# Hybrid decoder layer, gate/up stage: five blocks with four summed weight pairs, residual rows parked in HBM

## The chip, the cores and the metric

One core of a Trainium2 chip runs the whole layer in one launch. The metric is device time in microseconds; before the change it is 1085.96 us (median of 3 runs, 1085.82 to 1085.98).

## The reference

One decoder layer on x (256 tokens x 2048), everything in fp32:

```
u = RMSNorm(h)
lru_x, lru_gate, q, k, v, ret_gate = split(u @ W_in)          # 2048 x 6144
y = concat(RG-LRU(conv(lru_x)) * gelu(lru_gate),
           GroupNorm(retention(rope(q), rope(k), v)) * silu(ret_gate))
h = h + y @ W_out                                             # 2048 x 2048
h = h + (silu(u2 @ W_gate) * (u2 @ W_up)) @ W_down            # u2 = RMSNorm(h); 2048 x 5632 twice, 5632 x 2048
return RMSNorm(h)
```

With 256 tokens the layer is matrix products: 50 million weights are read once, and each product of two fp32 numbers is made of three TensorE products (hi x hi, hi x lo, lo x hi), for which every weight is split on the chip into a hi part (fp32r) and a lo part.

## The kernel before, in words

The kernel works off a list `program` of steps. Each step has weight units and a function that emits its matmuls. A loop at the end emits, ahead of each step, the loads of the steps to come (three loads ahead, `AHEAD`); `defer(n, f)` emits f after n further steps, `tick` counts them, one per step, empty steps included. What is emitted is then ordered per engine by a planner that works with a simulated timeline, so matmuls of neighbouring steps mix.

A load (512 KB, 128 x 1024) goes by SyncE's DMA queue into one of 6 `raw` buffers. `split` then makes the hi part (ScalarE cast, L112) and the lo part (VectorE subtraction, L113) in one of 4 `wh` and 4 `wl` buffers (or in tiles of 128 x 512 out of a pool of 60, `act_tile`).

From the output projection on (blocks 0 and 1), through gate/up (blocks 2 to 12, 512 columns of gate and the same of up each) to the down projection, a block holds four sums in four PSUM banks: c11, c12 (tokens 0 to 127 with the left and right 512 columns), c21, c22 (tokens 128 to 255). The 2048 rows of the weights come as 8 pairs of 128-row tiles. A pair is a 2 x 2 product, [a11 a12; a21 a22] with [b11 b12; b21 b22], and is done in one of two ways:

- plain, step "p": `EIGHT`, eight products of three matmuls (24 matmuls of 128 x 512), two loads;
- summed: seven products after Strassen and Winograd, of sums of activations (`Left`: s1 to s4) and sums of weights (t1 to t4, four VectorE sums per pair in `add`, L648). They are done apart: step "s" (`share`, two loads, 12 matmuls) for the products p1, p5, p6, p7, which are summed over the pairs, during the block before; step "d" (`direct`, one load of the second half again, 9 matmuls) in the block itself.

When the last pair is shared, L781 to L787 combine the four sums once per block: p1 is copied to a tile (ScalarE, L782), p and q are formed (VectorE, L783, L784), q goes to c12 (ScalarE, L785), and c22 and c21 are corrected (L786, L787). `direct` and `plain` then accumulate on these banks. `SUMMED` says which pairs of each block are summed, `STEPS` the order of its steps: the s steps in a block's string are the next block's pairs. The last step of a block ends its banks with `post`: silu and product (`ffn_post`, L842, L844), and the result is transposed on TensorE in the first step of the next block (`turn`, L833), for block 12 two steps later by `defer`.

The residual rows h (`htok`, 8 tiles of 128 x 512) are completed in blocks 0 and 1 by `out_post` (L585, L586) and stay in SBUF (`resid`) until the down projection adds to them (`into`, L888). The final norm's weights are loaded on SyncE's queue (`load_fw`, L861) into four `late` tiles. PSUM has two pools of four banks (`bank`, `aux`), used by odd and even blocks in turn (`room`).

## Time and profile before

| | before |
|---|---|
| runs, us | 1085.96 (1085.82 to 1085.98) |
| profiled execution: span from the first to the last instruction, us | 1084.4 |
| TensorE matmul busy | 1074.2 us, 99% |
| TensorE weight load busy | 899.5 us, 83% |
| VectorE busy | 953.5 us, 88% |
| ScalarE busy | 660.9 us, 61% |
| GpSimd busy | 51.0 us, 5% |
| HBM read, written | 235.26 MB, 2.10 MB |

The page gives the profiled execution's own time only as this span; the runs' median is 1.5 us above it. Rows begin with the engine or the line; an arrow points from the operands to the result; "x850" is a count. PE is TensorE, PEld its weight load, DVE VectorE, ACT ScalarE, POOL GpSimd, SP SyncE; a trailing q is the engine's queue. A matmul's own row is longer than its share of the pipeline, so what one costs is read from the starts of its neighbours.

### The profile page before, as it was taken

The page shows a single profiled execution, that of the slowest core. Times are in us where ns is not written, and L with a number is a line of the kernel's source. Part 1 is how long each engine was busy: PE and PEld are TensorE (multiplying, and loading weights), DVE is VectorE, ACT ScalarE, POOL GpSimd, SP SyncE. Part 2 cuts the span into 40 slices and gives each one's busy share as a digit, 9 for nine tenths or more (in the row PEclk, how much of TensorE's full clock was granted, in tenths as well). Part 3 has the DMA queues.
Part 4 walks back from the last instruction along what each step waited for, and adds up shares of the span by engine and source line. Part 5 has one row for each costly group of instructions (what it writes and reads, how often), then busy time and mean ns, then how long its engine had stood idle before and what let it go on. Part 6 is the DMA issues. An engine that isn't in the chain of part 4 may idle for free.

```text
span 1084.4 us, 14584 instructions
## 1 busy us (share of the span) xinstructions
PE 1074.2 (99%) x5101; PEld 899.5 (83%) x5101; DVE 953.5 (88%) x1371; ACT 660.9 (61%) x935; POOL 51.0 (5%) x61
## 2 busy tenths in 40 slices
PE   9999999999999999999999999999999999999997
PEld 7888888888888788888888888888888888888885
DVE  7789799988878889888998998999899899898986
ACT  7666644468746676565566566556556666655563
POOL 0612230000000000000000000000000000000001
PEclk9999999999999999999999999999999999999999
DMA  9964474444565567577677677686675756465652
GB/s 330 333 211 168 160 252 173 174 175 171 181 230 205 184 228 275 198 248 266 220 245 261 220 264 235 233 289 214 233 271 194 265 181 213 171 214 199 212 209 85
DMA packets 69274, 238.32 MB, mean 220 GB/s; under 512 B 7888, under 2 KB 8272, under 8 KB 69200
## 3 DMA queue, kind: packets, MB, share of 16 engines
q1 hardware_dynamic: 68400, 235.29, 62.7%
q0 software_dynamic: 512, 1.57, 0.4%
q8 instruction: 40, 0.66, 0.2%
q10 hardware_dynamic: 288, 0.52, 0.1%
q14 instruction: 34, 0.28, 0.1%
HBM read 235.26 MB, written 2.10 MB: 219 GB/s over the span
## 4 chain that ended last, share of the span: by engine, by line
PE 97%; DVE 1%; issue 1%; DMA 0%; ACT 0%; POOL 0%; SPq 0%; POOLq 0%; ACTq 0%
PE c L670 22%; PE c L672 22%; PE c L671 22%; PE fm L184 11%; PE fm L186 5%; PE tm L164 3%; PE tm L165 3%; PE tm L166 3%; PE p L672 1%; PE p L671 1%; PE p L670 1%; PE ft L833 1%; DMA raw<-in_w_v 0%; PE ht L576 0%; PE sc L482 0%
## 5 line engine op out<-in xcount | busy, mean ns | idle before, releaser
L112 ACT CAST wh<-raw 128x1024 fp32r<-128x1024 f32 (+1 forms) x490 | 460.9, 965 | 362.6 <-PE c L672 132.5
L113 DVE TENSOR_TENSOR wl<-raw,wh 128x1024 fp32r<-128x1024 f32 (+1 forms) x490 | 538.2, 1122 | 91.2 <-ACT wh L112 88.4
L671 PE MATMUL c<-wl,ah 128*128 128x512 f32 x850 | 331.0, 390 | 0.0
L672 PE MATMUL c<-wh,al 128*128 128x512 f32 x850 | 330.4, 389 | 0.0
L670 PE MATMUL c<-wh,ah 128*128 128x512 f32 x850 | 275.0, 391 | 0.2 <-ACT wh L112 0.2
L670 PEld LDWEIGHTS c<-wh,ah 128*128 128x128 f32 x850 | 159.4, 188 | 33.4 <-ACT wh L112 1.1
L672 PEld LDWEIGHTS c<-wh,al 128*128 128x128 f32 x850 | 159.6, 188 | 33.0
L671 PEld LDWEIGHTS c<-wl,ah 128*128 128x128 f32 x850 | 159.6, 188 | 32.7
L184 PE MATMUL fm<-u,wh 128*128 128x512 f32 x512 | 161.3, 396 | 0.0
L186 PEld LDWEIGHTS fm<-u,wl 128*128 128x128 f32 x512 | 96.0, 188 | 22.5
L186 PE MATMUL fm<-u,wl 128*128 128x256 f32 x512 | 101.1, 278 | 0.0
L184 PEld LDWEIGHTS fm<-u,wh 128*128 128x128 f32 x512 | 78.4, 189 | 0.3
L648 DVE TENSOR_TENSOR raw<-raw,raw 128x512 f32<-128x512 f32 x106 | 73.1, 690 | 2.8
L648 DVE TENSOR_TENSOR raw<-raw 128x512 f32<-128x512 f32 x106 | 72.7, 689 | 2.4
L671 PE MATMUL c<-wl,sh 128*128 128x512 f32 x176 | 68.5, 389 | 0.0
L672 PE MATMUL c<-wh,sl 128*128 128x512 f32 x176 | 68.0, 389 | 0.0
L670 PE MATMUL c<-wh,sh 128*128 128x512 f32 x176 | 60.4, 394 | 0.3 <-ACT sh L112 0.3
L165 PE MATMUL tm<-wl,u 128*128 128x512 f32 x128 | 48.8, 394 | 0.0
L166 PE MATMUL tm<-wh,u 128*128 128x512 f32 x128 | 48.7, 390 | 0.0
L164 PE MATMUL tm<-wh,u 128*128 128x512 f32 x128 | 47.3, 398 | 0.8 <-ACT u L288 0.8
L954 POOL TENSOR_TENSOR htok<-htok,fw 128x512 f32<-128x512 f32 x2 | 2.5, 1273 | 895.9 <-ACT junk L947 895.9
L670 PEld LDWEIGHTS c<-wh,sh 128*128 128x128 f32 x176 | 33.1, 188 | 7.3 <-ACT sh L112 0.7
(245 smaller groups left out, 1034.9 us busy)
## 6 DMA issues: line engine op xcount, KB each, us to landing
raw<-in_w_gu SPq DMA_DIRECT2D x212, 512.0 KB, 5.5
raw<-in_w_down SPq DMA_DIRECT2D x91, 512.0 KB, 4.3
raw<-in_w_out SPq DMA_DIRECT2D x34, 512.0 KB, 3.7
raw<-in_w_lx SPq DMA_DIRECT2D x16, 512.0 KB, 6.3
raw<-in_w_k SPq DMA_DIRECT2D x16, 512.0 KB, 3.5
raw<-in_w_q SPq DMA_DIRECT2D x16, 512.0 KB, 4.0
raw<-in_w_rg SPq DMA_DIRECT2D x16, 512.0 KB, 3.4
raw<-in_w_lg SPq DMA_DIRECT2D x16, 512.0 KB, 3.4
```

Of the source, the lines that this page charges most:

```text
L112: act.copy(out=dst_h, in_=src)
L113: v.tensor_tensor(out=dst_l, in0=src, in1=dst_h.bitcast(F32), op=ALU.subtract)
L164: pe.matmul(ps, ah, wh, start=first, stop=False)
L165: pe.matmul(ps, ah, wl, start=False, stop=False)
L166: pe.matmul(ps, al, wh, start=False, stop=last)
L184: pe.matmul(ps, wh, hl, start=n + i == 0, stop=False)
L186: pe.matmul(ps[:, :S], wl, hl[:, :S], start=False, stop=n + i == len(order) - 1)
L648: v.tensor_tensor(out=dst, in0=a, in1=b, op=ALU.add)
L670: pe.matmul(p, ah, bh, start=first, stop=False, skip_group_check=onto)
L671: pe.matmul(p, ah, bl, start=False, stop=False, skip_group_check=onto)
L672: pe.matmul(p, al, bh, start=False, stop=last, skip_group_check=onto)
L833: pe.transpose(pt[:, o : o + P], g[:, (2 * b + c) * P : (2 * b + c) * P + P], ident)
```

## The change

1. `SUMMED` and `STEPS`: blocks 4 to 8 have four summed pairs each (before, blocks 4, 6, 8 and 10 had four and the others three); blocks 4 to 7 run 4 p, 4 s and 4 d.
2. In those five blocks (`KEEP`) b11 and t2 are split into act tiles. `share` builds p1 in c22 (a11 x b11), copies it from there into c11's bank, which is one that a transposition of an earlier block wrote (`spare`), adds all pairs' s2 x t2 on top in c22 at the end, and combines with three VectorE sums and ScalarE copies. `share_apart` is the old way for the others.
3. s2 changes its sign (L552), and with it the forms of L783 and L898.
4. The four sums of a shared pair are no longer made together: the first at the load, the other three one by one with the next loads (`pending`).
5. The eight residual rows are written to HBM by ScalarE's queue in `out_post`; the `resid` pool and two others are closed ahead of block 3 (before: two pools, ahead of block 2) and six more raw buffers take the place, used every second load until block 12. After block 12 the rows come back, and the final norm's weights come, both on GpSimd's queue.
6. Transposes in gate/up set the accumulation flag on the first of a bank's four only.

```diff
-SUMMED = ((), (4, 5), (2, 3)) + ((1, 2, 3), (0, 1, 2, 3)) * 4 + ((1, 2, 3), (1, 2, 3))
+SUMMED = ((), (4, 5), (2, 3)) + ((1, 2, 3),) + ((0, 1, 2, 3),) * 5 + ((1, 2, 3), (0, 1, 2, 3), (1, 2, 3), (1, 2, 3))
-STEPS = ("pppspppspp", "ppspdpsdpp", "pdpsdpspspp") + ("pspsdpsdpsdp", "psdpsdpsddp") * 4 + ("psdpsdpsdpp", "psdpsdpsdpp")
+STEPS = ("pppspppspp", "ppspdpsdpp", "pdpsdpspspp") + ("pspsdpsdpsdp",) + ("psdpsdpsdsdp",) * 4 + ("psdpsdpsddp", "pspsdpsdpsdp", "psdpsdpsddp", "psdpsdpsdpp", "psdpsdpsdpp")
+KEEP = tuple(range(4, 9))
...
+    def raw_tile():
+        turn_of[0] += 1
+        pool_ = more[0] if more and turn_of[0] % 2 else rpool
+        return pool_.tile([P, 1024], F32, tag="raw", name=nm("raw"))
...
-                v.tensor_tensor(out=s2, in0=a11, in1=s1, op=ALU.add)
+                v.scalar_tensor_tensor(out=s2, in0=a11, scalar=-1.0, in1=s1, op0=ALU.mult, op1=ALU.subtract)
-                v.tensor_tensor(out=s4, in0=a12, in1=s2, op=ALU.subtract)
+                v.tensor_tensor(out=s4, in0=a12, in1=s2, op=ALU.add)
...
+            act.dma_start(out=kept[cb, t], in_=h)          # out_post, after the square
...
     class Shared(Quad):
-            self.add(r)
-            self.parts["t2"] = h[:, 512:], l[:, 512:]
-            split(*self.parts["t2"], r[:, :512])
-            self.cut(("t1", "t3"), self.ra)
             self.parts["t4"] = act_tile("t4h", F32R), act_tile("t4l", F32R)
-            split(*self.parts["t4"], r[:, 512:])
+            def first():
+                add(b11, b11, b12)
+            def second():
+                add(b12, b12, b22)
+                self.cut(("t1", "t3"), self.ra)
+            def third():
+                add(b22, b11, b22)
+                split(*self.parts["t2"], b22)
+            def fourth():
+                add(b21, b22, b21)
+                split(*self.parts["t4"], b21)
+            first()
+            pending.extend((self, f) for f in (second, third, fourth))
...
         def share(self, m):
+            ps, seed = self.ps, spare[self.index % 2]
+            if self.index not in KEEP:
+                return self.share_apart(m)
+            for c, a, b in (("c22", "a11", "b11"), ("c12", "s1", "t1"), ("c21", "s3", "t3")):
+                if m == 0:
+                    ps[c] = room(self.index)(c)
+                three(ps[c], left[a], right[b], m == 0, last)
+                if last and c == "c22":
+                    ps["c11"], spare[self.index % 2] = seed, None
+                    act.copy(out=seed, in_=ps["c22"])
+            if not last:
+                return
+            for k, i in enumerate(self.summed):
+                three(ps["c22"], self.lefts[i]["s2"], self.shared[k].parts["t2"], False, i == self.summed[-1], True)
+            p, q = act_tile("p"), act_tile("q")
+            act.activation(out=p, in_=ps["c22"], func=AF.Copy, scale=-1.0)
+            v.tensor_tensor(out=q, in0=p, in1=ps["c12"], op=ALU.subtract)
+            act.copy(out=ps["c12"], in_=q)
+            v.tensor_tensor(out=ps["c22"], in0=q, in1=ps["c21"], op=ALU.subtract)
+            v.tensor_tensor(out=ps["c21"], in0=ps["c21"], in1=p, op=ALU.subtract)
...
     def swap():
         early.close()
+        more.append(extra.enter_context(tc.tile_pool(name="raw2", bufs=6)))
+    def stop_more():                                       # ahead of block 12
+        more.clear()
+    def swap_back():                                       # after block 12
+        extra.close()
         late.append(ctx.enter_context(tc.tile_pool(name="late", bufs=4)))
+        resid[0] = ctx.enter_context(tc.tile_pool(name="resid2", bufs=8))
+        for key in [(cb, t) for cb in range(4) for t in range(2)]:
+            htok[key] = res_tile("htok")
+            pool.dma_start(out=htok[key], in_=kept[key])
+        load_fw()
...
+            if pending and pending[0][0] is not un:        # after each load
+                pending.pop(0)[1]()
+        while any(q in units for q, _ in pending):         # ahead of a step that needs them
+            pending.pop(0)[1]()
```

## Rows read from the trace of the kernel before

**Rows 1.** The page: busy line, and the chain by engine.

```profile
PE 1074.2 (99%) x5101; PEld 899.5 (83%) x5101; DVE 953.5 (88%) x1371; ACT 660.9 (61%) x935; POOL 51.0 (5%) x61
...
PE 97%; DVE 1%; issue 1%; DMA 0%; ACT 0%; POOL 0%; SPq 0%; POOLq 0%; ACTq 0%
```

**Rows 2.** Waits of PE: waiter <- cause: total us, times, longest.

```profile
PE warm L105 <- DVE eps_t L98: 1.1, 1, 1.1
...
PE c L670 <- ACT sh L112: 0.3, 1, 0.3
```

**Rows 3.** Order of time, PE, gate/up: start us, duration us, instruction, count.

```profile
559.73 0.39 PE L671 MATMUL c<-wl,ah 128*128 128x512 f32 x1
...
562.90 0.39 PE L671 MATMUL c<-wl,ah 128*128 128x512 f32 x1
...
575.14 1.30 PE L670 MATMUL c<-wh,ah 128*128 128x512 f32 x5
```

**Rows 4.** Windows of blocks 4, 5 and 12: us, busy of each engine, clock, DMA, GB/s.

```profile
477.20:516.20 39.00, 39.00 (x177) 32.32 (x176) 34.87 (x43) 23.36 (x32) 0.00 (x0) 1.00 0.72 247
516.20:561.30 45.10, 45.10 (x204) 37.38 (x203) 41.23 (x52) 26.51 (x35) 0.00 (x0) 1.00 0.73 244
...
811.20:853.20 42.00, 42.00 (x191) 34.60 (x190) 40.20 (x57) 28.40 (x39) 0.00 (x0) 1.00 0.64 225
```

**Rows 5.** Groups by line and shape: busy us, mean ns | idle before, releasers.

```profile
L113 DVE TENSOR_TENSOR wl<-raw,wh 128x1024 fp32r<-128x1024 f32 x392 | 477.7, 1231 | 78.4 <-ACT wh L112 75.8
...
L648 DVE TENSOR_TENSOR raw<-raw,raw 128x512 f32<-128x512 f32 x106 | 73.1, 690 | 2.8
...
L113 DVE TENSOR_TENSOR wl<-raw,wh 128x512 fp32r<-128x512 f32 x98 | 66.9, 683 | 12.7 <-ACT wh L112 12.5
...
L844 DVE SCALAR_TENSOR_TENSOR gated<-c,r_tok,gated 128x512 f32<-128x512 f32 x22 | 15.8, 741 | 0.6 <-ACT gated L842 0.6
...
L783 DVE TENSOR_TENSOR p<-c,p 128x512 f32<-128x512 f32 x13 | 8.9, 684 | 0.4 <-PE c L672 0.4
```

**Rows 6.** Order of time, ACT, around a copy of p1.

```profile
836.89 3.47 ACT L112 CAST wh<-raw 128x1024 fp32r<-128x1024 f32 x4
...
840.79 0.58 ACT L782 COPY p<-c 128x512 f32<-128x512 f32 x1
```

**Rows 7.** Waits of ACT from 400 to 800 us.

```profile
ACT wh L112 <- DVE raw L648: 87.3, 33, 3.0
ACT wh L112 <- PE c L672: 71.2, 62, 2.7
...
ACT wh L112 <- DMA raw<-in_w_gu: 0.2, 1, 0.2
```

**Rows 8.** DMA issues: ACT's (order of time), POOL's, and the gate/up loads (us to landing).

```profile
1079.31 0.88 ACTq L986 DMA_DIRECT2D out<-htok  x2
...
L441 POOL DMA_DIRECT2D decay<-in_decay x8: 556/562/772, 140.0 to 143.9; - x8
...
raw<-in_w_gu SPq DMA_DIRECT2D x212, 512.0 KB, 5.5
```

**Rows 9.** Order of time: PE near 370 and near 948 us.

```profile
370.41 0.50 PE L670 MATMUL c<-wh,ah 128*128 128x512 f32 x1
...
371.78 0.39 PE L671 MATMUL c<-wl,sh 128*128 128x512 f32 x1
...
947.95 0.39 PE L672 MATMUL p<-wh,sl 128*128 128x512 f32 x1
...
950.20 0.40 PE L671 MATMUL p<-wl,sh 128*128 128x512 f32 x1
```

**Rows 10.** Line L888: duration ns min/median/max, first and last start.

```profile
L888 DVE TENSOR_TENSOR htok<-htok,part x8: 680/682/685, 953.6 to 1062.5; 128x512 f32<-128x512 f32 x8
```

**Rows 11.** Order of time after block 12: its last products, and their transposes.

```profile
854.59 1.40 DVE L844 SCALAR_TENSOR_TENSOR gated<-c,r_tok,gated 128x512 f32<-128x512 f32 x2
...
859.76 0.38 PE L833 MATMUL ft<-ident,gated 128*128 128x128 f32 x2
```

More of the change, by code (lines that the diff above doesn't have):

```diff
@@ L124, in load @@
         def load(self, j):
-            raw = rpool.tile([P, 1024], F32, tag="raw", name=nm("raw"))
+            raw = raw_tile()
             h = wpool.tile([P, 1024], F32R, tag="wh", name=nm("wh"))
@@ L146, in part @@
             return self.h[j][:, o : o + cw], self.l[j][:, o : o + cw]
-    halfway = []
+    halfway, pending = [], []
     program = []
@@ L566, in tile_hymba_layer @@
     turns = []
+    kept = nc.dram_tensor("kept_rows", (4, 2, P, 512), F32, kind="Internal").ap()
     def out_post(d):
@@ L626, in load @@
         def load(self, half):
-            r = rpool.tile([P, 1024], F32, tag="raw", name=nm("raw"))
+            r = raw_tile()
             nc.sync.dma_start(out=r, in_=self.src[:, half * 1024 : half * 1024 + 1024])
@@ L721, in block, with transposes @@
         program.append((quads[n:], end))
+    spare = [None, None]
+    def transposes(pt, parts):
+        for n, x in enumerate(parts):
+            pe.matmul(
+                pt[:, n * P : n * P + P], x, ident, start=n == 0, stop=True, is_transpose=True, skip_group_check=n > 0
+            )
     class Shared(Quad):
-        hl = None, None
+        keep = False
         def load(self, half):
-            r = rpool.tile([P, 1024], F32, tag="raw", name=nm("raw"))
+            r = raw_tile()
             nc.sync.dma_start(out=r, in_=self.src[:, half * 1024 : half * 1024 + 1024])
@@ L732, in load, with add @@
                 self.before()
-            h, l = self.hl
             if half == 0:
                 self.ra = r
-                h, l = self.hl = [wpool.tile([P, 1024], F32R, tag=g, name=nm(g)) for g in ("wh", "wl")]
-                self.parts["b11"] = h[:, :512], l[:, :512]
+                if self.keep:
+                    self.parts["b11"] = act_tile("b11h", F32R), act_tile("b11l", F32R)
+                else:
+                    h, l = (wpool.tile([P, 1024], F32R, tag=g, name=nm(g)) for g in ("wh", "wl"))
+                    self.parts["b11"], self.parts["t2"] = ((h[:, c : c + 512], l[:, c : c + 512]) for c in (0, 512))
                 split(*self.parts["b11"], r[:, :512])
                 return
-            self.add(r)
-            self.parts["t2"] = h[:, 512:], l[:, 512:]
-            split(*self.parts["t2"], r[:, :512])
-            self.cut(("t1", "t3"), self.ra)
+            if self.keep:
+                self.parts["t2"] = act_tile("t2h", F32R), act_tile("t2l", F32R)
             self.parts["t4"] = act_tile("t4h", F32R), act_tile("t4l", F32R)
-            split(*self.parts["t4"], r[:, 512:])
+            b11, b12, b22, b21 = self.ra[:, :512], self.ra[:, 512:], r[:, :512], r[:, 512:]
+            def add(dst, a, b):
+                v.tensor_tensor(out=dst, in0=a, in1=b, op=ALU.add)
+            def first():
[11 more added lines that the diff above has]
+            pending.extend((self, f) for f in (second, third, fourth))
     class Direct(Quad):
@@ L756, in load @@
         def load(self, half):
-            r = rpool.tile([P, 1024], F32, tag="raw", name=nm("raw"))
+            r = raw_tile()
             nc.sync.dma_start(out=r, in_=self.src[:, 1024:2048])
@@ L768, in __init__, with share_apart @@
             self.shared = [Shared(src(i), True, before and (lambda i=i: before(i))) for i in self.summed]
+            for q in self.shared:
+                q.keep = index in KEEP
             self.ps = {}
         def share(self, m):
+            left, right, last = self.lefts[self.summed[m]], self.shared[m].parts, m == len(self.summed) - 1
+            ps, seed = self.ps, spare[self.index % 2]
[18 more added lines that the diff above has]
+            v.tensor_tensor(out=ps["c21"], in0=ps["c21"], in1=p, op=ALU.subtract)
+        def share_apart(self, m):
             left, right, last = self.lefts[self.summed[m]], self.shared[m].parts, m == len(self.summed) - 1
@@ L782, in share @@
             act.copy(out=p1, in_=ps["c11"])
-            v.tensor_tensor(out=p, in0=ps["c12"], in1=p1, op=ALU.subtract)
+            v.scalar_tensor_tensor(out=p, in0=ps["c12"], scalar=-1.0, in1=p1, op0=ALU.mult, op1=ALU.subtract)
             v.tensor_tensor(out=q, in0=p, in1=ps["c22"], op=ALU.subtract)
@@ L829, in turn @@
             pt = room(j)("ft")
-            for c in range(2):
-                for t, g in enumerate(gated):
-                    o = c * S + t * P
-                    pe.transpose(pt[:, o : o + P], g[:, (2 * b + c) * P : (2 * b + c) * P + P], ident)
+            transposes(pt, [g[:, (2 * b + c) * P : (2 * b + c) * P + P] for c in range(2) for g in gated])
+            if b and j + 4 in KEEP:
+                spare[j % 2] = pt
             ff[2 * j + b] = act_tile("ff")
```

20 lines of the change are left out of this document (12 added, 8 removed).

## The prediction

> **What bounds the kernel now.** I read the page's busy line and its chain first: TensorE is busy 99% of the span, it holds 97% of the chain that ended last, and its granted clock is 1.00, the upper of its two levels (2.4 GHz), in every window of this stage [rows 1, 4]. Busy is not peak, so I asked next who makes TensorE wait: in 1084.4 us the list names four causes, 1.1 us the longest and 0.3 us the longest at a product of the later stages [rows 2]. The order of time then shows how tightly matmuls follow each other: from 559.73 to 562.90 us there are 14 intervals, 3.17 us, 0.2265 us per matmul of 128x512 [rows 3]. The windows by gate/up block close the account. A block is a list of steps, p (24 matmuls), s (12) and d (9). One with 5 p, 4 s, 3 d has 195 matmuls and takes 45.1 us, one with 4 p, 3 s, 4 d has 168 and takes 39.0 us [rows 4]; 27 matmuls are 6.1 us, 0.226 each, and what is left over both 195 x 0.2265 = 44.2 and 168 x 0.2265 = 38.1 is 0.9 us, the eight transposes. So the time of a gate/up block is its count of matmuls, with nothing added. VectorE is second, 89.4% and 91.4% in those two blocks, ScalarE far behind [rows 4].
>
> **Two more summed pairs.** SUMMED counted per block gives 3, 4, 3, 4, 3, 4, 3, 4, 3, 3 for blocks 3 to 12 before and 3, 4, 4, 4, 4, 4, 3, 4, 3, 3 after: blocks 5 and 7 gain one pair each. A plain pair costs one p = 24 matmuls; a summed one s + d = 12 + 9 = 21. So 2 x 3 = 6 matmuls go, 6 x 0.2265 = 1.36 us, on the path. In blocks: blocks 4 to 7 are the two of rows 4 twice over, 39.0 + 45.1 + 39.0 + 45.1 = 168.2 us; four blocks of 4 p, 4 s, 4 d have 180 matmuls, 180 x 0.2265 + 0.9 = 41.7 us each, 166.8 together.
>
> On VectorE each such exchange adds four sums (4 x 0.69) and three half splits (3 x 0.68): 4.8 us. The two whole splits of p, 2 x 1.23, are replaced by those of s and d, 2 x 1.23 [rows 5]. That is 9.6 us in all, six half casts on ScalarE, and one load of 512 KB each. All of it lies beside matmuls, if VectorE has room. A 4 p, 4 s, 4 d block takes it 41.23 us less one split (1.0 by spacing to 1.23) less one combination sum (0.69), 39.3 to 39.5, or from the other block 34.87 + 2.76 + 2.05 + 1.23 - 0.69 = 40.2: 94 to 96% of 41.7 us. Is that too much? The block from 811.2 to 853.2 us already has VectorE at 40.20 of 42.0 us, 95.7%, and TensorE at 42.00 of 42.00 [rows 4]. So I cost it at nothing, and what it costs without that cover is the slower rival below.
>
> **Combination with one sum less.** In the five blocks 4 to 8 the product p1 is built in c22 and copied by ScalarE into c11's bank (instead of into a tile); the sum p1 + p6 comes out of accumulation and ScalarE's copy with scale -1 stands for VectorE's L783. VectorE saves 5 x 0.684 = 3.4 us, ScalarE gets 5 x 0.58 = 2.9 us more [rows 5, 6], TensorE's count is the same. One wait is new: the s2 x t2 matmuls of c22 must stay behind ScalarE's copy out of c22. Between them lie six matmuls (c12 and c21), 1.36 us. The copy itself is 0.58 us, but ScalarE works its queue in order, and such a copy has stood behind a run of casts that began 840.79 - 836.89 = 3.9 us before it [rows 6]. The bounds are therefore nothing (copy reached at once, or matmuls of other steps put between) and 3.9 + 0.58 - 1.36 = 3.1 us a block, 16 us in all. I take nothing, by the nearest row: in the combination of before TensorE waits for ScalarE in no gate/up block [rows 2, 4]. Queued behind it would be every later matmul.
>
> **Signs.** TENSOR_TENSOR becomes SCALAR_TENSOR_TENSOR in L552, L783 (eight blocks) and L898. At 128x512 with a PSUM operand the two kinds cost 684 and 741 ns [rows 5]: some 10 x 0.06 = 0.6 us on VectorE for the last two, at L552's quarter of the size no more each, and nothing on the path.
>
> **Sums between other work, and buffers.** The four sums of a pair ran as one group, and ScalarE waited 87.3 us for them in 400 us; for gate/up weights to land it waited 0.2 us [rows 7]. So six more raw buffers remove no wait of TensorE's; they hold what the postponed sums keep longer. Gain and loss on the path: 0, where 0.7 us is the bound for the gain (the stall at 370 us, below).
>
> **The residual rows.** Eight stores issued by ScalarE, 0.44 us each on its queue by the two stores at the end [rows 8], 3.5 us in blocks 0 and 1, and no wait, since the square ahead waited for the same sum. A gain is excluded, they only add; at the other end four of them (1.8 us) lie ahead of the chain to the stall at 370 us, so up to 1.8 us; I take 0, since ScalarE works 61% of its time [rows 1] and sits idle for sums and buffers in between [rows 7]. Coming back: 8 rows and 4 weight rows of 256 KB, issued by GpSimd at about 0.56 us each [rows 8], 6.7 us of an engine that is busy 5% in all [rows 1]. They wait for the last readers of the six buffers, early in block 12, and are needed from 953.6 us on [rows 10], more than 100 us later. They add 3.1 MB to a stretch that moves 225 GB/s at a DMA share of 0.64 [rows 4]: 5 to 14 us during which weight loads share; those land 5.5 us after issue [rows 8], and in block 12 six buffers serve them as before. Bounds 0 and 2 us, taken 0.
>
> **The empty step.** swap_back is one more step between block 12 and the down projection, so the transposes of the last gate/up tiles, put off by two steps, are emitted one step earlier. Before, their input was ready at 854.59 + 1.40 = 855.99 us and they ran at 859.76 [rows 11]. Put straight behind the last matmul of the block they would wait up to 2.6 us; I take 0: they ran 3.8 us after their input was ready, so other matmuls were at hand for that long.
>
> **Sum.** -1.36 us on the path, all else beside it: the profiled execution, span 1084.4 us, becomes 1083.0. The runs' median lies 1.5 us above that span and I carry that over: 1085.96 - 1.36 = 1084.6 us. By the Trainium skill (TensorE: Matmul & The Clock Gate, section Back-to-back issue gap) a sustained matmul of 512 columns costs about 131 ns, by which the six would be worth 0.8 us and the time an estimated 1085.2; the trace shows 0.2265 us over every such stretch, and the measurement decides.
>
> **The rivals.**
> *VectorE becomes the bound (slower).* Place: blocks 4 to 7. If VectorE can't be kept busier than the 90.4% it shows on average over the two kinds of block there, 39.8 us of work make a block of 44.0 us instead of 41.7: 4 x 2.3 - 1.4 = 7.8 us, 1093.8 us. It decides from a reachable share of 94.7% downwards (39.8 / 0.947 = 42.0 us eats the gain); at 93.5% the kernel is 0.2% slower. For it: up to five matmuls with hi parts run in a row while lo parts are being made [rows 3], and 95% with ScalarE in the loop leaves little. Against: the 95.7% block, and that ScalarE waited 71.2 us in 400 us for TensorE to free split buffers, so the preparation is ahead [rows 4, 7]. Chance 0.14. It is the way the Trainium skill would point (Perfetto Trace Analysis, section Identifying the Most-Contended Engine): matmul busy share is no measure, the weight loads' share is, and these are at 83%, below VectorE's 88% [rows 1], so the kernel's most contended engine would be the one that gets more work. The spacing of rows 3 speaks against that reading here.
>
> *New waits eat the gain.* The copy wait of five blocks at 0.5 us each, or one of the 2 us bounds above: 1085.2 to 1087.5 us. For it the in-order queue of rows 6; against it that no gate/up block shows any such wait. Chance 0.14.
>
> *Existing stalls go too (faster).* Near 370 us three intervals take 1.37 us instead of 0.68, and ahead of 950.20 us six take 2.25 instead of 1.36 [rows 9]; ScalarE stood behind sums in the first. Both gone: 1085.96 - 1.36 - 0.69 - 0.89 = 1083.0 us. For it the spread sums; against, the second lies in the down projection, whose sums aren't spread. Chance 0.20.
>
> *The forecast*, 1083.6 to 1085.2 us: 0.52.
>
> **From this the numbers.** 0.2% is 2.2 us, about what a measurement of this kernel can tell from no change: below 1083.8 is faster, above 1088.1 slower. Faster: 0.20 and the forecast's lower edge, 0.05: 0.25. Slower: the VectorE rival, 0.14. The rest, 0.61, is the same. The range leaves out about 0.05 below and 0.14 above: 1082.7 to 1088.1.
>
> **What would show it.** Right: TensorE's gate/up blocks 4 to 7 at 41.7 us each, six matmuls fewer, VectorE near 95% there, the list of TensorE's waits no longer than now. Wrong: TensorE idle behind L112 or L113 in these blocks (VectorE bound), behind the copy into c11's bank (new wait), behind weight DMAs near 820 us, or a wait of the ft transposes near 853 us. A time under 1083.8 would mean that something off the count of matmuls was worth more than I see.

## The result: 0.37% slower, outside the range

The changed kernel takes 1090.12 us (median of 5 runs, 1088.90 to 1091.05) against 1085.96 us (5 runs, 1085.71 to 1087.17) on the same chip. The ratio is 1.0037, with a 95% interval of 1.0025 to 1.0050: slower by 4.2 us, where 1.36 us less was forecast, and 2.0 us above the upper end of the range. The profiled span went from 1084.4 to 1088.6 us, the same 4.2.

First the page of after: the busy line, and the chain by engine, which answer to [rows 1].

```profile
PE 1074.4 (99%) x5095; PEld 897.6 (82%) x5095; DVE 955.3 (88%) x1380; ACT 666.6 (61%) x946; POOL 57.3 (5%) x73
...
PE 92%; DVE 3%; DMA 2%; issue 1%; ACT 1%; POOL 0%; SPq 0%; POOLq 0%; ACTq 0%
```

The six matmuls are gone (5101 to 5095). But the chain, 97% TensorE before, now runs through VectorE (3%), a DMA (2%) and ScalarE (1%). The waits of TensorE between 360 and 960 us name the places; the longest of them from block 2 on was 0.3 us before [rows 2].

```profile
PE c L681 <- ACT wh L120: 1.7, 3, 1.4
PE c L681 <- DVE c L835: 1.6, 3, 0.8
PE c L682 <- DVE wl L121: 1.0, 1, 1.0
```

A wait in this list is shorter than what it costs (0.8 us here, 1.08 us by the starts, at 564 us). So from here on a loss is read from the starts of neighbouring matmuls: what an interval has beyond 0.2265 us [rows 3]. All losses over 0.3 us from 330 us on, worked out so from the traces:

| | last matmul starts, against before | losses: place in us and size |
|---|---|---|
| before | 1076.32 | 370: 0.69; 389: 0.37; 948: 0.87 |
| after | +4.14 | 371: 1.36; 411: 1.62; 564: 1.08; 607: 0.62; 649: 1.08; 844: 0.44; 952: 0.86 |

The account: -1.36 (matmuls) + 0.67 (371) + 1.62 (411) + 2.78 (ends of blocks 5, 6 and 7) + 0.44 - 0.37 = +3.8. Near 340 us after is 0.34 us ahead, so it falls 4.5 us behind from there on; the other 0.7 us lies in losses below 0.3 us and in transposes. Two places carry most of it. The first is the order of time of after at 371 and 411 us, on four engines (start, duration, instruction; in brackets the idle time before it and what ended that).

```profile
371.45 1.21 PE L681 MATMUL c<-wh,ah 128*128 128x512 f32 x4
373.63 0.50 PE L682 MATMUL c<-wl,ah 128*128 128x512 f32 x1 [0.97 <-DVE wl L121]
...
396.59 0.33 SPq L639 DMA_DIRECT2D raw<-in_w_gu  x1
...
399.93 0.66 SPq L750 DMA_DIRECT2D raw<-in_w_gu  x1
401.87 2.06 SPq L639 DMA_DIRECT2D raw<-in_w_gu  x2
403.42 1.76 ACT L120 CAST wh<-raw 128x1024 fp32r<-128x1024 f32 x2 [0.63 <-PE c L683]
...
410.50 1.42 DVE L768 TENSOR_TENSOR raw<-raw,raw 128x512 f32<-128x512 f32 x2 [3.25 <-DMA raw<-in_w_gu]
411.80 2.52 ACT L120 CAST wh<-raw 128x1024 fp32r<-128x1024 f32 x3 [6.62 <-DMA raw<-in_w_gu]
412.89 1.20 PE L681 MATMUL c<-wh,ah 128*128 128x512 f32 x4 [1.35 <-ACT wh L120]
```

At 371 us a lo part is late. At 411 ScalarE sat 6.62 us and VectorE 3.25 us without work, for a load; SyncE had issued seven loads in 3.3 us just ahead of it, when the new buffers came open. The DMA view of 390 to 415 us, before and then after (last number: median us from issue to landing):

```profile
raw<-in_w_gu SPq DMA_DIRECT2D x10, 512.0 KB, 5.4
```

```profile
raw<-in_w_gu SPq DMA_DIRECT2D x14, 512.0 KB, 9.0
```

The second place is the end of blocks 5 to 7, here block 5:

```profile
562.71 0.39 PE L683 MATMUL c<-t2h,sl 128*128 128x512 f32 x1
...
563.14 0.60 ACT L832 ACTIVATE p<-c 128x512 f32<-128x512 f32 x1 [1.67 <-PE c L683]
...
563.77 0.69 DVE L833 TENSOR_TENSOR q<-p,c 128x512 f32<-128x512 f32 x1 [1.04 <-ACT p L832]
...
564.38 0.68 DVE L121 TENSOR_TENSOR b11l<-raw,b11h 128x512 fp32r<-128x512 f32 x1
...
564.98 0.69 DVE L835 TENSOR_TENSOR c<-q,c 128x512 f32<-128x512 f32 x1
...
565.72 0.50 PE L681 MATMUL c<-wh,ah 128*128 128x512 f32 x1 [0.81 <-DVE c L835]
```

It is a chain: the last product of s2 x t2 into c22, ScalarE's copy p, VectorE's q, a split that stands between, the corrected c22, and only then the next matmul into c22. From the last product to that matmul are 3.0 us, and beside them lie only the eight matmuls into c11's bank, 1.8 us. ScalarE sat idle for 1.67 us before p and VectorE for 1.04 us before q, so what is late here is the chain, not a VectorE without room; the gate product comes only at 566.18 us, after TensorE's wait.

### The profile page after: what moved, and what is told of

Read it like the earlier page. It is cut to its first block, busy times and chain, and to the rows that moved or that the text cites. A ratio compares the mean times of both kernels' runs of the same rounds, so it can differ in the third digit from the quotient of the medians.

```text
span 1088.6 us, 14590 instructions
## 1 busy us (share of the span) xinstructions
PE 1074.4 (99%) x5095; PEld 897.6 (82%) x5095; DVE 955.3 (88%) x1380; ACT 666.6 (61%) x946; POOL 57.3 (5%) x73
## 4 chain that ended last, share of the span: by engine, by line
PE 92%; DVE 3%; DMA 2%; issue 1%; ACT 1%; POOL 0%; SPq 0%; POOLq 0%; ACTq 0%
PE c L681 20%; PE c L682 20%; PE c L683 20%; PE fm L192 11%; PE fm L194 5%; PE tm L172 3%; PE tm L174 3%; PE tm L173 3%; DMA raw<-in_w_gu 2%; PE ft L681 1%; DVE wl L121 1%; PE ft L682 1%; PE ft L683 1%; PE p L683 1%; PE p L682 1%
## 5 line engine op out<-in xcount | busy, mean ns | idle before, releaser
L120 ACT CAST wh<-raw 128x1024 fp32r<-128x1024 f32 (+1 forms) x454 | 441.2, 993 | 347.2 <-PE c L683 119.0
L121 DVE TENSOR_TENSOR wl<-raw,wh 128x1024 fp32r<-128x1024 f32 (+1 forms) x454 | 516.5, 1156 | 82.1 <-ACT wh L120 79.3
L682 PE MATMUL c<-wl,ah 128*128 128x512 f32 x758 | 295.1, 390 | 1.0 <-DVE wl L121 1.0
L683 PE MATMUL c<-wh,al 128*128 128x512 f32 x758 | 295.0, 390 | 0.0
L681 PE MATMUL c<-wh,ah 128*128 128x512 f32 x758 | 245.5, 391 | 3.4 <-ACT wh L120 1.7
L681 PEld LDWEIGHTS c<-wh,ah 128*128 128x128 f32 x758 | 142.0, 188 | 35.2 <-ACT wh L120 3.3
L682 PEld LDWEIGHTS c<-wl,ah 128*128 128x128 f32 x758 | 142.3, 188 | 30.8 <-DVE wl L121 1.6
L683 PEld LDWEIGHTS c<-wh,al 128*128 128x128 f32 x758 | 142.3, 188 | 29.3
L768 DVE TENSOR_TENSOR raw<-raw,raw 128x512 f32<-128x512 f32 x86 | 58.2, 688 | 4.8 <-DMA raw<-in_w_gu 3.3
L172 PE MATMUL tm<-wh,u 128*128 128x512 f32 x128 | 46.8, 394 | 0.8 <-ACT u L296 0.8
L683 PEld LDWEIGHTS c<-wh,sl 128*128 128x128 f32 x164 | 30.8, 188 | 6.4
```

The costliest lines, as they stand in the source:

```text
L120: act.copy(out=dst_h, in_=src)
L121: v.tensor_tensor(out=dst_l, in0=src, in1=dst_h.bitcast(F32), op=ALU.subtract)
L172: pe.matmul(ps, ah, wh, start=first, stop=False)
L681: pe.matmul(p, ah, bh, start=first, stop=False, skip_group_check=onto)
L682: pe.matmul(p, ah, bl, start=False, stop=False, skip_group_check=onto)
L683: pe.matmul(p, al, bh, start=False, stop=last, skip_group_check=onto)
```

## The experiments

Each kernel ran with before on the same chip, 4 to 11 executions each; the losses are read as above, from one profiled execution. The theories weighed: A: a burst of loads at the moment the buffers open is late. B: VectorE has too much work for a block of 41.7 us. C: spreading a pair's sums holds raw buffers longer, too long while only six exist. D: the combination is a chain of latencies that outlasts the matmuls beside it, whatever VectorE's load. E: four pairs of split buffers end VectorE's lead. F: VectorE has room, but its work lies too densely at certain points.

### Which part costs what

**x5_pairs_only**: before with the two tables `SUMMED` and `STEPS` alone.

> The kernel before with the change's table of pairs and steps alone: six matmuls less, nothing else. Theories A and D, and the forecast's main step: blocks 4 to 7 at 41.7 us, no new wait of TensorE, 1085.96 - 1.36 = 1084.6 us. Theory B (VectorE is the bound at 94 to 96%): waits behind L112 and L113 in blocks 4 to 7, 1087 us or more.

1089.01 us, ratio 1.0029 (1.0018 to 1.0041). The two more summed pairs, all by themselves, cost 3.26 us against before in the same runs (1085.75); in the trace the last matmul starts 2.88 us later. Four blocks lose 0.43 in the middle (510, 553, 596, 639 us) and 0.65 at the end (520, 563, 606, 649). The window of block 5 (VectorE's busy time is the third, 40.16 us), and the order of time in it:

```profile
521.40:564.20 42.80, 42.35 (x190) 34.23 (x189) 40.16 (x51) 25.87 (x34) 0.00 (x0) 1.00 0.74 248
```

```profile
549.88 0.69 DVE L648 TENSOR_TENSOR raw<-raw 128x512 f32<-128x512 f32 x1
...
550.60 1.42 DVE L648 TENSOR_TENSOR raw<-raw,raw 128x512 f32<-128x512 f32 x2
...
551.40 2.95 ACT L112 CAST wh<-raw 128x1024 fp32r<-128x1024 f32 x3 [3.42 <-DVE raw L648]
...
552.05 0.69 DVE L648 TENSOR_TENSOR raw<-raw 128x512 f32<-128x512 f32 x1
552.66 2.35 DVE L113 TENSOR_TENSOR wl<-raw,wh 128x1024 fp32r<-128x1024 f32 x2
...
553.46 0.50 PE L670 MATMUL c<-wh,ah 128*128 128x512 f32 x1 [0.16 <-ACT wh L112]
...
562.47 0.68 DVE L784 TENSOR_TENSOR q<-p,c 128x512 f32<-128x512 f32 x1
...
563.19 0.59 ACT L785 COPY c<-q 128x512 f32<-128x512 f32 x1 [0.83 <-DVE q L784]
...
563.83 0.50 PE L670 MATMUL c<-wh,ah 128*128 128x512 f32 x1 [0.29 <-ACT c L785]
```

The block takes 42.8 us where 41.7 were forecast. In the middle the fourth s step's four sums come as one group: ScalarE idles 3.42 us for them, and its casts reach TensorE late. (In after, with the sums spread, ScalarE idles the same 3.42 us at 545.87 and TensorE does not wait; its idle time alone does not decide.) At the end the combination is late: TensorE waits for the copy of q.

**x10_old_table**: after with the two tables of before, so everything but the two pairs.

> The changed kernel with the old table of pairs and steps (blocks 4, 6 and 8 with four pairs, 5 and 7 with three): everything else of the change is in. Theory B: the combination waits of blocks 5, 6 and 7 go (2.8 us), the waits of the postponed sums at 372 and 411 us stay (2.3 us more than before): 1085.96 + 2.3 = 1088.3 us. Theory D (the new combination's order itself): the waits at block ends stay: 1091 us or more.

1088.87 us, 1.0025 (1.0016 to 1.0034). Only the losses at 371 (1.37) and 411 (1.27) are left; no block end waits. So those two do not come from the pairs.

**y3_spread_late**: x10, with a pair's sums spread only once the six buffers are open (A keeps the loss at 411, C takes it away).

```diff
-            pending.extend((self, f) for f in (second, third, fourth))
+            if more:
+                pending.extend((self, f) for f in (second, third, fourth))
+            else:
+                second()
+                third()
+                fourth()
```

> The changed kernel with the old table (1088.9 us), and the sums spread only from the moment on when the six additional raw buffers are open; before that they are made together. Theory C (the spread sums cost the waits at 372 and, in part, 411 us): 372 back to 0.7 us, 411 down to the 0.8 us that the run with sums together and six more buffers had: 1087 us. Theory A (burst of loads alone): 411 stays at 1.3 us: 1088 us.

1087.42 us, 1.0010 (1.0001 to 1.0018); the losses are those of before (0.69, 0.37, 0.87) and the last matmul starts where it did (-0.02 us). So spreading ahead of time makes them; by the ratios of the runs it costs 1.6 us (1.0025 against 1.0010). At 371 us that is clear: all five profiles with it (after, x1, x3, x7, x10) lose 1.36 us or 1.37 there, and those with the sums together 0.69 (x8, with GpSimd sums, 0.91). At 411 us it is not the only cause: x2, y4 and z1 do without it and still lose 0.80, 0.99 and 0.50.

**y4_parked_and_comb**: x10 with the sums together and no new buffers, so the parked rows, the new combination and the signs.

```diff
-            pending.extend((self, f) for f in (second, third, fourth))
+            add(b12, b12, b22)
...
-        more.append(extra.enter_context(tc.tile_pool(name="raw2", bufs=6)))
```

> The changed kernel with the old table, sums together and no additional raw buffers: what is left of the change is the parking of the residual rows, the combination with one sum less in blocks 4 to 8 and the signs. The forecast's zeros for these: 1085.9 us, within 0.3. Rival (stores by ScalarE, the copy into c11's bank, or 3.1 MB coming back in block 12 cost time): 1086.5 us or more, with the wait at 340 to 390, at block ends, or at 820 us.

1086.77 us, 1.0007 (0.9998 to 1.0016). No difference that can be told, and at 371 us, behind the stores, the 0.69 of before. Its profiled execution was the slowest of its eleven (1088.54) and loses 0.95 us at 44, 0.35 at 381 and 0.99 at 412.

### The loss at 411 us

**x1_no_raw2**: after with the six buffers never opened.

```diff
-        more.append(extra.enter_context(tc.tile_pool(name="raw2", bufs=6)))
```

> The changed kernel with its six raw buffers alone: the residual rows still go to HBM and come back, but the freed space stays empty. Theory A (the stall of 1.6 us at 411 us comes from a burst: six free buffers let ten loads be issued in 10 us, so that the load needed next lands 9.8 us after its issue): the stall at 411 us is gone, the three combination waits of 0.6 to 1.1 us at the ends of blocks 5, 6 and 7 (2.8 us together) stay: 1088.5 us. Theory C (the stall comes from the postponed sums, which hold raw buffers longer): the stall stays or grows, as there are fewer buffers now: 1090 us or more.

1095.77 us, 1.0103 (1.0086 to 1.0119). By A the loss at 411 would go with the burst. It stays (1.74 us in two parts) and others come: 2.70 at 523, 2.35 at 567, 0.97 and 1.32 after. The spread sums hold their buffers, the next load is issued late, and ScalarE waits for it:

```profile
524.40 1.04 ACT L120 CAST wh<-raw 128x1024 fp32r<-128x1024 f32 x1 [3.64 <-DMA raw<-in_w_gu]
```

A alone falls: spread sums and only six buffers are enough, and y3 issues the same burst (16 loads, 7.4 us to land in the median, from 390 to 415 us) and loses nothing at 411. Whether the burst adds its share there stays open.

**x2_sums_together**: after, a pair's four sums at the load, as before.

```diff
-            pending.extend((self, f) for f in (second, third, fourth))
+            second()
+            third()
+            fourth()
```

> The changed kernel with the four sums of a shared pair made together at the load again; all else stays, the six additional raw buffers too. Theory A (burst of loads): the stall near 411 us stays within 0.5 us, the combination waits stay: 1089.5 to 1090.5 us. Theory C (postponed sums): the stall near 411 us is gone: 1088.5 us. Forecast's view that the spread sums are worth up to 0.7 us near 370 us: a stall there that is larger than the 1.4 us of the changed kernel.

1093.86 us, 1.0075 (1.0062 to 1.0088). The loss at 371 is back at 0.69 and the one at 411 halves (0.80). But blocks 5 to 7 now lose 0.93 in the middle and 1.75 at the end, each. The one in the middle, in block 5:

```profile
550.69 0.57 ACT L827 COPY ft<-c 128x512 f32<-128x512 f32 x1 [4.61 <-PE c L683]
...
551.32 0.50 PE L681 MATMUL c<-t2h,sh 128*128 128x512 f32 x1 [0.66 <-ACT ft L827]
```

That is the wait that the prediction bounded between 0 and 3.1 us and took at 0: the s2 x t2 products behind ScalarE's copy out of c22. In after it does not show: ScalarE's copy starts at 550.22 and the first of these products at 553.19, with other matmuls between.

**z4_spread_late**: after, with y3's edit.

> The changed kernel, the sums spread only once the six additional raw buffers are open (together before that). All theories: the waits at 372 and 411 us are back at 0.7 and 0; the three combination waits of blocks 5, 6, 7 stay: 1090.1 - 2.3 = 1087.8 us.

1088.64 us, 1.0023 (1.0013 to 1.0032). 371 is back at 0.69, 411 is gone, and the block ends stay to the digit (1.08, 0.62, 1.08). A new loss of 1.50 at 381 us, behind a load, stands in no other of these traces at this size (z3 has 1.00 there, y4 and y1 0.35 and 0.34); I have no cause for it.

### The block ends

**x3_old_comb**: after with `KEEP = ()`, so the old combination.

> The changed kernel with the old combination (p1 copied to a tile, four VectorE sums) in all blocks; five blocks with four pairs stay. Theory D (the waits at the ends of blocks 5, 6, 7 come from the new order: all s2 x t2 products last, then a copy, two sums and the bank of c22): these waits are gone, -2.8 us: 1087.3 us, although VectorE gets 3.4 us more work. Theory B (VectorE is the bound in blocks 4 to 7): the waits stay or grow by 0.7 us a block: 1090 us or more.

1089.84 us, 1.0040 (1.0027 to 1.0054). Four ends lose 0.63 each, 2.5 us in all; the new combination loses 2.78 at three ends. In size the two hardly differ. The middle of the blocks, 0.43 four times in x5 with this same combination and table, is now free. Of what x3 has beyond x5, the stores, the reload and the signs cost and gain nothing that can be told (y4); what is left is spreading the sums over more buffers.

**x7_last_s_early**: after, in blocks 4 to 7 the last s step two steps earlier.

```diff
-("psdpsdpsdsdp",) * 4
+("psdpsdsdspdp",) * 4
```

> The changed kernel with the steps of blocks 4 to 7 in the order psdpsdsdspdp instead of psdpsdpsdsdp: the last s comes 24 matmuls, 5.4 us, earlier, so the combination has 57 instead of 33 matmuls behind it. Theory D (a chain of latencies after the last s2 x t2): the waits at the block ends go, 2.8 us: 1087.3 us. Theory B (VectorE's work): they move to the split of the pairs, inside the block: 1089.5 to 1091 us.

1090.79 us, 1.0042 (1.0029 to 1.0055). The ends are free, and 0.93 to 0.99 us appear in the middle (506, 549, 592, 634), again behind the copy into c11's bank, as the waits of TensorE between 360 and 960 us say. The loss moves with the step.

```profile
PE c L681 <- ACT ft L825: 2.7, 4, 0.7
```

**y1_pairs_no_gate_product**: x5 without VectorE's product of silu(gate) and up (L844); the output is that of silu(gate) alone.

```diff
-            v.scalar_tensor_tensor(out=gated[t], in0=ps, scalar=r, in1=gated[t], op0=ALU.mult, op1=ALU.mult)
```

> The kernel before with the change's table of pairs and steps (1089.0 us), and the product of gate and up left out (two VectorE operations of 0.74 us a block; the gated tile is silu(gate) alone). This takes 1.5 us a block off VectorE, 40.2 to 38.7 us, and touches neither the sums and splits of weights nor the combination. Theory B (VectorE's load sets the pace): VectorE falls to 92 to 93% of a 41.7 us block, the waits of 1.08 us a block in blocks 4 to 7 go: 1084.7 us. Theory D (latency of the combination and of the four sums, whatever VectorE's load): they stay: 1088.5 to 1089 us.

1087.81 us, 1.0014 (1.0005 to 1.0023). The end losses are gone, the 0.43 in the middle stays in all four blocks:

```profile
518.90:561.10 42.20, 42.04 (x190) 34.40 (x189) 39.05 (x49) 25.71 (x35) 0.00 (x0) 1.00 0.74 249
```

VectorE is at 39.05 / 42.2 = 92.5%, and in the middle TensorE still waits for casts that wait for its sums. At the end of block 5, where x5's TensorE waits until 563.83 for the copy of q:

```profile
562.45 0.68 DVE L784 TENSOR_TENSOR q<-p,c 128x512 f32<-128x512 f32 x1
...
563.16 0.59 ACT L785 COPY c<-q 128x512 f32<-128x512 f32 x1 [0.83 <-DVE q L784]
...
563.36 0.38 PE L833 MATMUL ft<-ident,gated 128*128 128x128 f32 x2
563.49 0.48 PE L670 MATMUL c<-wh,ah 128*128 128x512 f32 x1
```

The sum q and its copy run when they ran in x5 (562.47 and 563.19). What is new is TensorE's order: transposes, which in x5 wait for the gate product (563.67) and come at 565.33, fill the gap. So the end is not cured by a VectorE that gets there earlier. (Two new losses, 0.60 at 1003 and 0.50 at 1014 us, belong to the down projection.)

### Is VectorE full?

**y2_vector_burden** and **z3_burden_tied** were to load VectorE in before by 36 instructions more.

```diff
+                if half and self.burden:
+                    v.tensor_tensor(out=sumsq[:, :S], in0=sumsq[:, :S], in1=sumsq[:, :S], op=ALU.max)   # y2
+                    v.tensor_tensor(out=sumsq[:, :S], in0=r[:, :S], in1=r[:, :S], op=ALU.max)           # z3
```

> The kernel before, with its own table, and one VectorE operation of 128x256 on an unused tile (0.42 us) for each plain pair in blocks 4 to 11: 4 to 5 a block, 1.9 us, on no path of data. VectorE's share goes from 90.4 to 95%, TensorE's matmuls stay as they are. Theory B: waits of about 1 us a block appear, 8 us in all: 1093 us (1090 to 1095). Theory D, and the prediction's reading of the 95.7% block: nothing appears: 1085.9 us.

> The kernel before with its own table, and one VectorE operation of 128x256 (0.42 us) that reads the raw buffer of each plain pair in blocks 4 to 11, 1.9 us a block; its result is not used. VectorE's share in these blocks goes from 90.4 to about 95%, matmuls and steps stay. Theory B (VectorE's load as such): waits of 0.5 to 1 us a block, 4 to 8 us in all: 1090 to 1094 us. Theory F (where the work lies: two s with no p between, and combination, gate products and first sum together at the block's end): no waits of TensorE, 1086 us.

Both missed. In y2 (1085.88 us, 0.9999, 0.9990 to 1.0008) the planner put all 36 between 46.8 and 117.3 us, where nobody waits. In z3 they read the load, and were placed right behind it: VectorE, which works in order, waited for transfers. Its waits from 480 to 690 us:

```profile
DVE sumsq L635 <- DMA raw<-in_w_gu: 29.3, 15, 3.4
```

1127.20 us, 1.0375 (1.0360 to 1.0389): 41 us for 36 short instructions, and nothing learned on load.

**x8_fourth_sum_pool**: x5 with the fourth sum of each shared pair on GpSimd.

```diff
-                v.tensor_tensor(out=dst, in0=a, in1=b, op=ALU.add)
+                (fourth if dst is b21 else v).tensor_tensor(out=dst, in0=a, in1=b, op=ALU.add)
```

> The kernel before with the change's table of pairs and steps, and the fourth sum of each shared pair made by GpSimd instead of VectorE: 4 x 0.69 us a block off VectorE, 40.2 to 37.4 of 42.8 us. Theory B (VectorE at 94% sets the pace in blocks 4 to 7): the waits of 1.08 us a block go, 4.3 us in all: 1089.0 - 4.3 = 1084.7 us. Theory E (not VectorE's load but the split buffers, four pairs, end its lead): the waits stay, 1089 us. Rival G: GpSimd takes 1.3 to 1.7 us for such a sum and t4 comes late: over 1089 us, with waits behind t4.

1097.17 us, 1.0102 (1.0089 to 1.0115), 8 us worse than x5. The groups by shape from 480 to 690 us show why; first the GpSimd sums of the whole kernel, then VectorE's splits in that stretch:

```profile
L648 POOL TENSOR_TENSOR raw<-raw 128x512 f32<-128x512 f32 x43 | 56.4, 1311 | 619.6 <-DVE raw L648 337.4 <-DMA fw<-in_final_norm_w 129.9 <-DMA raw<-in_w_gu 73.6
...
L113 DVE TENSOR_TENSOR wl<-raw,wh 128x1024 fp32r<-128x1024 f32 x77 | 107.2, 1418 | 14.9 <-ACT wh L112 14.9
```

A sum takes GpSimd 1.31 us (VectorE 0.69), and VectorE's splits rose from 1231 ns [rows 5] to 1418 on the mean, the longest of them to 2.07 us: 77 x 0.19 = 14.4 us given back for about 19 sums x 0.69 = 13 us taken off (19 shared pairs fall into the stretch).

**x9_split_buffers**: after with the old combination, the sums together, and the space used for three more pairs of `wh` and `wl`.

```diff
-        more.append(extra.enter_context(tc.tile_pool(name="raw2", bufs=6)))
+        more.append(extra.enter_context(tc.tile_pool(name="split2", bufs=3)))
```

> The changed kernel with the old combination, the sums made together, and the space of the residual rows given to three more pairs of split buffers instead of six raw buffers. VectorE's work per block is that of the table alone (40.2 us). Theory E (four pairs of split buffers end VectorE's lead): the waits of blocks 4 to 7 go, 1084.7 us. Theory B (VectorE's work itself): a longer lead saves only the first waits, 1 us in all at most: 1088 to 1089 us.

1094.37 us, 1.0078 (1.0064 to 1.0093). Nearly 8 us are lost between 520 and 531 us, behind casts of ScalarE, one of which waited 2.7 us for a load; what more split buffers would do for the ends it does not tell.

**z1_late_oldcomb_gatepool** and **z2_late_gatepool**: z4 with the gate product by a ScalarE copy and a GpSimd product, z1 with the old combination (`KEEP = ()`), z2 with the new.

```diff
-            v.scalar_tensor_tensor(out=gated[t], in0=ps, scalar=r, in1=gated[t], op0=ALU.mult, op1=ALU.mult)
+            up = act_tile("up")
+            act.activation(out=up, in_=ps, func=AF.Copy, scale=r)
+            pool.tensor_tensor(out=gated[t], in0=up, in1=gated[t], op=ALU.mult)
```

> The changed kernel with late spreading, the old combination, and the product of gate and up moved from VectorE to ScalarE (a scaled copy out of PSUM, 0.7 us) and GpSimd (the product of two tiles, 1.3 us), same result. 1.5 us a block leave VectorE. Theories B and F: the four waits of 0.63 us at the block ends go, and with spread sums there is none inside the block: 1085.96 - 1.36 = 1084.6 us, below the kernel before. Theory D (the combination's own chain of latencies): the waits stay: 1087 us.

> As the kernel before it in this list, with the new combination in blocks 4 to 8. Theory D (the s2 x t2 products last, then copy, sum, sum): waits of 0.6 to 1.1 us at three block ends stay, 1087.4 us. Theories B and F: they go, 1084.6 us. Rival: one or two tiles more in a pool of 60 that is nearly full cost waits of ScalarE for tiles: above 1088 us.

z1: 1096.13 us, 1.0090 (1.0076 to 1.0103): ends of 0.91 us in four blocks, where B and F wanted none (x3, with the gate product on VectorE, has 0.63), and some 6 us in block 12. z2: 1091.01 us, 1.0041 (1.0027 to 1.0055): no loss at all in blocks 4 to 7, and some 6 us in block 12, where it starts so. First the order of time of z2, then its splits from 809 to 819 us (ns min/median/max):

```profile
815.20 0.54 POOL L934 DMA_DIRECT2D fw<-in_final_norm_w  x1 [0.24 <-ACT wh L120]
815.75 2.51 POOL L917 TENSOR_TENSOR gated<-up,gated 128x512 f32<-128x512 f32 x2
819.41 0.50 PE L682 MATMUL c<-wl,ah 128*128 128x512 f32 x1 [1.98 <-DVE wl L121]
```

```profile
L121 DVE TENSOR_TENSOR wl<-raw,wh x4: 683/955/3868, 808.9 to 815.5; 128x512 fp32r<-128x512 f32 x2, 128x1024 fp32r<-128x1024 f32 x2
```

The products of block 11 stand behind GpSimd's reload DMAs, and a split of VectorE's that lies beside them takes 3.87 us instead of 0.68.

**z6_gatepool_middle**: z2 with this product on GpSimd for `2 <= j <= 6` only (the gate/up columns of blocks 4 to 8), VectorE's instruction for the others.

```diff
+            if 2 <= j <= 6:
                 up = act_tile("up")
                 act.activation(out=up, in_=ps, func=AF.Copy, scale=r)
                 pool.tensor_tensor(out=gated[t], in0=up, in1=gated[t], op=ALU.mult)
+            else:
+                v.scalar_tensor_tensor(out=gated[t], in0=ps, scalar=r, in1=gated[t], op0=ALU.mult, op1=ALU.mult)
```

> Kernel after, the sums of a group spread only once the six buffers are open (as z4), and the gate product of the five groups of columns that end blocks 4 to 8 (after 476 us, up to 690 us) made by a ScalarE copy and a GpSimd product; from block 9 on it stays with VectorE, so nothing of it stands behind GpSimd's reload DMAs at 809 us. Theory (it matters where VectorE's work lies at a block's end, and the six matmuls then come out whole): blocks 4 to 7 without a gap (41.7 us each), no wait in block 12, so 1085.96 - 1.36 and the 0.8 us that z4's wait near 381 us may still cost: 1084 to 1086 us, ratio 0.998 to 1.000. Rival (VectorE is simply full and the work that leaves one block comes late in the next): 1088 to 1090 us as z4_spread_late, with waits of VectorE in block 8 or 12. If block 12 stretches again as in the version with all products on GpSimd (6 us), the reload DMAs were not its cause: 1090 to 1092 us.

1085.37 us, 0.9995 (0.9986 to 1.0004), where after stands at 1.0037. Its losses past 330 us are those of before (0.69, 0.37, 0.87), and its last matmul starts 1.08 us earlier than before's. Its windows of blocks 5 and 12 and its order of time at the end of block 5:

```profile
518.60:560.40 41.80, 41.80 (x190) 34.59 (x189) 39.15 (x48) 27.29 (x38) 3.00 (x2) 1.00 0.72 240
...
809.20:851.50 42.30, 42.30 (x192) 34.94 (x191) 40.30 (x58) 28.14 (x38) 5.93 (x12) 1.00 0.85 288
```

```profile
558.70 0.39 PE L683 MATMUL c<-t2h,sl 128*128 128x512 f32 x1
...
559.40 0.59 ACT L837 ACTIVATE p<-c 128x512 f32<-128x512 f32 x1
...
560.68 0.68 DVE L838 TENSOR_TENSOR q<-p,c 128x512 f32<-128x512 f32 x1
...
561.28 0.69 DVE L121 TENSOR_TENSOR b11l<-raw,b11h 128x512 fp32r<-128x512 f32 x1
...
561.88 0.69 DVE L840 TENSOR_TENSOR c<-q,c 128x512 f32<-128x512 f32 x1
...
562.33 1.29 POOL L918 TENSOR_TENSOR gated<-up,gated 128x512 f32<-128x512 f32 x1 [38.76 <-ACT up L917]
...
562.48 0.69 DVE L841 TENSOR_TENSOR c<-c,p 128x512 f32<-128x512 f32 x1
...
562.79 0.40 PE L681 MATMUL c<-wh,ah 128*128 128x512 f32 x1
563.08 1.09 DVE L768 TENSOR_TENSOR raw<-raw 128x512 f32<-128x512 f32 x1
```

The chain has the steps of after's, and it is not shorter: 3.9 us from the last product (558.70) to the corrected c22 (561.88 + 0.69), against 2.96 in after. What changed is TensorE's order, which the planner makes: the last product comes nine matmuls earlier, 17 matmuls lie between it and the next one into c22, not 8, and the corrected c22 is there when TensorE comes to it. z4, which differs in the gate product alone, has 8 there, and its gate product too runs after the correction (565.81 against 564.61). The count between the last product and the next matmul into c22 puts the ends in order:

| ends | matmuls beside the chain | lost, us |
|---|---|---|
| x2, 563 and 608 us | 5 | 1.75, 1.76 |
| after and z4, 564 and 649 us | 8 | 1.08 |
| x2, 652 us (the gate product runs inside the chain, which takes 3.6 us) | 9 | 1.80 |
| after and z4, 607 us | 10 | 0.62 |
| x2, 520 us | 11 | 0.40 |
| x10, all five | 13 or more | 0 |
| z6, blocks 4 to 6 | 17 | 0 |

A chain of 2.96 us (after) is 13 matmuls of 0.2265 us, and each one fewer costs about that much. Block 5 of z6 has the 190 matmul rows of x5's in 41.8 us instead of 42.8. This is the forecast's own block.

## Why the prediction was wrong

**The matmuls: right.** 5101 became 5095, and where nothing waits the four-pair block takes the 41.7 us forecast (z6: 41.7, 41.8, 41.8, 41.2 for blocks 4 to 7, 166.5 together; 166.8 were forecast).

**The step that failed: "All of it lies beside matmuls, if VectorE has room", costed at nothing on the strength of one block with VectorE at 95.7% [rows 4].** x5 makes that step alone and loses 4 x (0.43 + 0.65) = 4.3 us, against 1.36 gained. The sum of VectorE's work was right (39.3 to 40.2 us forecast; after's two blocks with 190 matmul rows have 39.44 and 40.29); the inference from a share was wrong. At 92.5% TensorE still waits in the middle of a block (y1), at 93.5% in blocks 4 to 7 and 95.3% in block 12 it does not (z6). What decides is where the work stands and what TensorE has beside it: in the middle four sums in one group just ahead of the casts that need them (2.8 us of sums, ScalarE idle for 3.42); at the block's end the combination, a chain of 3.0 us on three engines while TensorE has 1.8 us of other matmuls (after). With four p steps instead of five, two s steps follow each other with only a d, no p's 24 matmuls, between; no run puts a p back there, so its share is not shown. By the Trainium skill (Perfetto Trace Analysis, section Identifying the Most-Contended Engine) the engine with the highest occupancy is the one to optimize first. That is VectorE here, 88% against the weight loads' 83%, and in the traces its share did not say where TensorE waits: VectorE sits idle for 1.04 us inside after's late chain, and z1 takes the gate product off it and loses more at the ends than x3.

**The rival "VectorE becomes the bound"** had place and sign right, and I gave it 0.14. Its size does not test it: with the 93.8% that x5 reached (40.16 / 42.8) its formula must give back x5's own block of 42.8 us. Its reason (a ceiling of VectorE's share) is not shown, and at the ends the traces speak against it: VectorE waits inside the chain (after), and what z6 and y1 change is TensorE's order. Still, z6 also takes VectorE from 40.16 to 39.15 us a block, so load and place were not parted cleanly; the two runs that were to load VectorE alone missed. That a lighter VectorE lets the planner find the better order stays a possibility.

**Spread sums and buffers: "Gain and loss on the path: 0" failed twice.** I looked at what the postponed sums hold and at the buffers, but not at when: the list of steps starts spreading in block 0, the buffers open ahead of block 3. Without spreading ahead of time the losses at 371 and 411 us go (y3): 2.1 us of the 4.2 by the two traces (last matmul of x10 +2.09, of y3 -0.02), 1.6 by the ratios of the runs; part of the loss at 411 us comes without it too (x2, y4). From there on the pair is worth something that I had put at 0 as well: it takes away the 0.43 in the middle of the blocks (x3 against x5).

**The new combination: 0 taken, bounds 0 to 3.1 us a block.** It costs 0.9 us a block in three blocks. But the wait is another than the one I bounded: not the s2 x t2 products behind ScalarE's copy (that one shows in x2 and x7, 0.93 to 0.99 a block), but everything behind these products, because they come last. With the old table the same combination loses nothing at the ends (x10), where 13 matmuls or more lie beside it. With the old combination the pairs lose 2.5 us instead of 2.8 (x3), so as against before's it is worth nothing here.

**Signs, stores, reload, empty step: 0, right as far as it can be told.** y4 has all of them and stands at 1.0007 (0.9998 to 1.0016). The growth of the stall at 370 us is not the stores': x2 and y4 have them and are back at 0.69.

**What stays open.** y3's last matmul starts as early as before's, and yet the median of its eleven runs lies 1.2 us above before's (1.0010, 1.0001 to 1.0018); the profiled execution is one of the fastest of them (1086.34), and what the others lose is not seen. Losses behind loads at 381 and 411 us come and go between traces, and their cause is open. Why the planner's order has 8 matmuls in one kernel and 17 in another is open. z6 carries the same parts, and by the median gains 0.5 us of the 1.36. In its profile 0.43 us are lost at 44 us, in a stage that the change does not touch. z6 is below before by less than can be told from no change.

## What to carry over

A share of busy time, even one that another stage sustains, is no proof of room: ask how long the chain is from the last product to the matmul that needs its correction, and whether the engine that waits has that much other work just then: count the matmuls that its order puts there. When a change opens more buffers and also holds each longer, see that the second does not begin before the first. When moving work off a busy engine cures a wait, compare the order of the other engines before calling the load its cause; and look at what stands ahead of the work in the helper's queue.

## What the runs showed of the hardware

- GpSimd and VectorE slow each other. Beside GpSimd's products and sums of two SBUF tiles, VectorE's two-input instructions on SBUF took longer: a sum 1.09 us instead of 0.69 (z6 at 563.08), a split 3.87 instead of 0.68 (z2), whole splits 1418 ns instead of 1231 on the mean (x8); those with a PSUM operand kept their 0.69 (z6 at 562.48). Two such products took GpSimd 2.51 us (z2 at 815.75) to 3.44 (z6 at 645.81). The Trainium skill (SBUF — State Buffer, section SBUF: two separate sides) says that the two share a port pair which one holds for a whole instruction, also against VectorE instructions with two SBUF inputs. The traces agree in kind: a split of 0.68 us and the two products' 2.51 are 3.19 of the 3.87 us; the rest is not explained.
- 36 short VectorE instructions placed right behind the loads that they read cost 41 us (z3): VectorE waited 29.3 us for transfers at them from 480 to 690 us alone.
- From 390 to 415 us, 14 loads of 512 KB, seven of them issued in 3.3 us, took 9.0 us to land (median); ten in the same stretch of before took 5.4.
